# Four edits at the start of a decoder layer: the norm's row in a zeroed tile, filler products, the sample tile eighth, and each tile's sums behind the next tile's splits

## The chip, the core and the metric

The kernel runs on one core of a Trainium2 chip. The engines are PE (TensorE: products and transposes into PSUM), DVE (VectorE), ACT (ScalarE), POOL (GpSimd) and SP (SyncE, which here only issues loads). The metric is the device time of one execution in microseconds (us), as a median of runs.

## The reference

One layer of a recurrent decoder on 1024 new prompt tokens and 8 sample tokens. What matters here is its beginning:

```python
hn = rmsnorm(x, g_norm)                     # x * rsqrt(mean(x*x) + EPS) * g_norm, 1024 features
u = hn @ w_in                               # 1024 x 7176, in float32
xa, za, uq, uk, uv, uo, zb, ui, uf = jnp.split(u, SPLIT_IDX, axis=-1)
```

Then come an RG-LRU branch on `xa`, an mLSTM on `uq, uk, uv, ui, uf`, gates from `za, uo, zb`, a product with `w_out`, the residual and a last norm. Prompt and sample tokens go through the same weights; the sample has states of its own.

## The kernel before, in words

**Precision.** A float32 operand is split into two parts, `hi` (a cast on ACT, L72) and `lo = src - hi` (a subtraction on DVE, L73); `mm3` makes a product of three: hi x hi, hi x lo, lo x hi (L66 to L68).

**Token tiles.** The prompt's 1024 tokens are eight tiles of 128 (numbers 0 to 7), the eight sample tokens are tile 8. `xorder` sets the order, here 4, 0, 8, 5, 1, 6, 2, 7, 3. For each tile: `x_fetch` loads its 512 KB (the sample: 32 KB) three places ahead; `x_stats` (ACT's Square, a few small operations) makes the row scale; `x_turn` scales it by that and by the norm's gain `gn_b` on DVE (L439) and transposes it in eight 128x128 blocks on PE (L443); `x_split` splits the transposed halves (`b12` and `cb` of the page, for tiles 4 to 7 and 0 to 3); `plain` multiplies the tile with two groups of weight columns, w = 0 (with the gate columns, 264 wide, weights `wph`/`wpl`) and w = 1 (256 wide, `w1h`/`w1l`); and `x_combos` makes sums and differences of token halves and splits them too. They are the seven operand pairs `cb[q]` of a Strassen-like scheme (seven products of half-size blocks instead of eight), in which all other weight columns are multiplied. For the sample, `x_split` only copies the transposed tokens to `hnd`.

**The norm's row.** `g_norm` is loaded as one row, in two halves (`grow`), and spread to 128 partitions by a product with a column of ones (L537, one row deep, 512 columns each). The first tile takes it from PSUM, all others from the copy `gn_b`.

**Units.** The weight columns come in 14 units of 2 x 256 columns. A unit's raw weights are two buffers, `raw0` (rows 0 to 511) and `raw1`, of which there is one each: the next unit's load (`load_raw`, L244) must wait until the unit before has been read for the last time. Unit 0 is the one that `plain` multiplies. For every unit, `dec_unit` multiplies the sample (`hnd`) with the raw weights: eight products (L257) in a PSUM buffer `ps_tr`, of which there is one, then a copy `Z` on ACT. `prep` splits a unit's weights for one of the seven products (`wh`, `wl`), `product` makes it.

**Order.** The program is written in the order shown; a scheduler places each engine's instructions, and each engine then runs them strictly in order. `tc.issue_after(i)` keeps the instructions of a block behind `i` where they run on its engine. `dec_unit(0)` can run when `hnd` is there, so with the sample third it stands early. ACT and DVE run ahead with `prep` of unit 1 as soon as its raw weights are there.

Of the kernel before, what the change touches and what calls it, by code (L numbers as in the profile page):

```python
# [9 lines left out]
F32 = mybir.dt.float32  # L10
F32R = mybir.dt.float32r
BF16 = mybir.dt.bfloat16
AF = mybir.ActivationFunctionType
ALU = mybir.AluOpType
# [3 lines left out]
P = 128  # L18
T = 1024
HT = 512  # L20
NB = 8
KC = 8
# [29 lines left out]
def hymba_kernel(  # L52
# [7 lines left out]
    V, A, G, TE = nc.vector, nc.scalar, nc.gpsimd, nc.tensor  # L60
# [3 lines left out]
    def mm3(out, ah, al, bh, bl, first, last):  # L64

        TE.matmul(out, ah, bh, start=first, stop=False, skip_group_check=True)  # L66
        TE.matmul(out, ah, bl, start=False, stop=False, skip_group_check=True)  # L67
        TE.matmul(out, al, bh, start=False, stop=last, skip_group_check=True)  # L68

    def split(hi, lo, src):  # L70

        a = A.copy(hi, src)  # L72
        V.tensor_tensor(lo, src, hi.bitcast(F32), op=ALU.subtract)  # L73
        return a

    cpool = ctx.enter_context(tc.tile_pool(name="cpool", bufs=1))
    dram = ctx.enter_context(tc.tile_pool(name="dram", bufs=1, space=DRAM))
# [4 lines left out]
    def ps(tag, shape):  # L82
        return psp.tile(shape, F32, tag=tag, name=f"ps_{tag}", bufs=NBUF.get(tag, 1))

    def const(shape, name, dt=F32):
        return cpool.tile(shape, dt, tag=name, name=name)
# [14 lines left out]
    def sg(shape, name, dt=F32):  # L101

        return stg.tile(shape, dt, tag="stg", name=name)
# [4 lines left out]
    def dconst(shape, name):  # L108

        return dpool.tile(shape, F32, tag=name, name=name)  # L110
# [4 lines left out]
    ones = dconst([P, P], "ones")  # L115
# [102 lines left out]
    def blocks(t):  # L218
        return t[:, 0:KC * NB].rearrange("p (k b) -> p k b", b=NB)
# [164 lines left out]
        stq(d[t0:t0 + 256, :].rearrange("(i p) c -> p i c", p=P), t.rearrange("p (i c) -> p i c", i=2))  # L384


    grow = [sg([1, HT], f"grow{half}") for half in range(2)]
    for half in range(2):
        A.dma_start(grow[half], g_norm[:, half * HT:(half + 1) * HT])
    warm = const([P, 1], "warm")  # L390
    A.activation(warm, ones[:, 0:1], AF.Sqrt)
    es_f = ExitStack()
    fp = es_f.enter_context(tc.tile_pool(name="f_start", bufs=1))
    gn_b = fp.tile([P, T], F32, tag="gn_b", name="gn_b")
    xorder = [4, 0, 8, 5, 1, 6, 2, 7, 3]
    rows_of = lambda i: P if i < 8 else NB
    xt, xps, bf = {}, {}, {}

    def x_fetch(m):
        i = xorder[m]  # L400
        xt[i] = fp.tile([P, T], F32, tag="xb", name=f"x{i}") if m % 3 == 2 else ws([P, T], f"x{i}", F32)
        ld(xt[i][:rows_of(i)], x_prompt[0, i * P:(i + 1) * P, :] if i < 8 else x_sample[:, 0, :])
# [21 lines left out]
    def x_stats(i):  # L424
        n = rows_of(i)
        junk = fp.tile([P, T], BF16, tag="junk", name="junk")
        A.activation(junk[:n], xt[i][:n], AF.Square, accum_out=st0[:n, i, 0:1])
        rsqrt_mean(st0[:n, i, 1:2], st0[:n, i, 0:1], st0[:n, i, 2:3], T)

    def x_turn(m):  # L430
        i = xorder[m]
        n = rows_of(i)
        xps[i] = []
        for half in range(2):
            hs = slice(half * HT, (half + 1) * HT)
            if m == 0 or half == 0:
                s = hs if m == 0 else slice(0, T)
                g = pb[half] if m == 0 else gn_b[:n, s]
                scaled = V.scalar_tensor_tensor(xt[i][:n, s], xt[i][:n, s], st0[:n, i, 1:2], g, op0=ALU.mult, op1=ALU.mult)  # L439
            pt = ps(("kv", "kv", "s", "qp")[(2 * m + half) % 4], [P, 4, P])  # L440
            for q in range(4):
                k = half * 4 + q
                TE.transpose(pt[:, q, 0:n], xt[i][:n, k * P:(k + 1) * P], idF[:n, :n])  # L443
            xps[i].append(pt)
        del xt[i]
        return scaled

    def x_split(i, half):

        p = xps[i][half]  # L450
        if i == 8:
            V.tensor_copy(blocks(hnd)[:, 4 * half:4 * half + 4], p[:, :, 0:NB])
            return
        s = slice(i % 4 * P, (i % 4 + 1) * P)
        if i >= 4 and half == 0:
            bf[i] = [fp.tile([P, 4, P], F32R, tag=f"b12{n}", name=f"b12{n}") for n in "hl"]
            split(*bf[i], p)
        else:
            q = Q_P3 if i >= 4 else (Q_P1, Q_P2)[half]
            return split(cb[q][0][:, :, s], cb[q][1][:, :, s], p)  # L460

    def x_copy(i):

        bf["f"] = [sg([P, 4, P], f"b{n}2f") for n in (1, 2)]
        for f, p in zip(bf["f"], xps[i]):
            A.copy(f, p)

    def x_combos(i):

        p0, p1 = xps[i]  # L470
        s = slice(i % 4 * P, (i % 4 + 1) * P)
        f0, f1 = bf["f"]

        def out(q, t):
            split(cb[q][0][:, :, s], cb[q][1][:, :, s], t)
        if i >= 4:
            t3 = sg([P, 4, P], "t3")
            V.tensor_tensor(t3, f1, f0, op=ALU.subtract)
            out(Q_P7, t3)
        else:  # L480
            t1, t2, t4 = (sg([P, 4, P], f"t{n}") for n in (1, 2, 4))
            V.tensor_tensor(t1, f0, p0, op=ALU.subtract)
            V.tensor_tensor(t2, f1, t1, op=ALU.subtract)
            V.tensor_tensor(t4, p1, t2, op=ALU.subtract)
            out(Q_P6, t2)
            out(Q_P5, t1)
            out(Q_P4, t4)

    hi = fp.tile([P, KC, 264], F32R, tag="wph", name="wph")
    lo = fp.tile([P, KC, 264], F32R, tag="wpl", name="wpl")  # L490
# [3 lines left out]
    def w1_split(b):  # L494

        t = ws([P, 4, 256], f"w1h{b}"), ws([P, 4, 256], f"w1l{b}")
        split(t[0], t[1], raws[0, b][:, :, 256:512])
        w1.append(t)
# [3 lines left out]
    def plain(i):  # L502

        s = slice(i % 4 * P, (i % 4 + 1) * P)
        op = []
        for k in range(KC):
            if i < 4:
                op.append([t[:, k % 4, s] for t in cb[Q_P1 if k < 4 else Q_P2]])
            elif k < 4:
                op.append([t[:, k, :] for t in bf[i]])  # L510
            else:
                op.append([t[:, k % 4, s] for t in cb[Q_P3]])
        for w in range(2):
            pt = ps("o", [P, 512])[:, 0:264 - 8 * w]
            for k, (h, l) in enumerate(op):
                wh, wl = (hi[:, k, :], lo[:, k, :]) if w == 0 else (t[:, k % 4, :] for t in w1[k // 4])
                mm3(pt, h, l, wh, wl, k == 0, k == KC - 1)
            t = fp.tile([P, 256], F32, tag="pe", name="pe", bufs=2)
            A.copy(t, pt[:, 0:256])
            if w == 0:  # L520
                V.tensor_tensor(gs[:, i, :], pt[:, 256:264], bgate, op=ALU.add)
            stq(d_v[w][i * P:(i + 1) * P, :], t)

    pw = ps("tr", [P, P])
# [9 lines left out]
        TE.matmul(pw, ones, ones, start=True, stop=True)  # L534
    pb = [ps("o", [P, 512]) for half in range(2)]
    for half in range(2):
        TE.matmul(pb[half], ones[0:1, :], grow[half], start=True, stop=True)  # L537
    ld(wg, w_in[0, :, C_G:C_G + 8].rearrange("(k p) c -> p k c", p=P))
    load_raw(0, 1, (0,))
    x_fetch(1)  # L540
# [6 lines left out]
    for m, i in enumerate(xorder):  # L547
        scaled = x_turn(m)
        if m == 0:
            def w0_split(k):  # L550
                split(hi[:, k:k + 2, 0:256], lo[:, k:k + 2, 0:256], raws[0, k // 4][:, k % 4:k % 4 + 2, 0:256])
            with tc.issue_after(root.ins), tc.issue_after(scaled.ins):
                w0_split(0)
                split(hi[:, :, 256:264], lo[:, :, 256:264], wg)
                x_split(i, 0)
                w0_split(2)
            with tc.issue_after(x_split(i, 1).ins):
                w0_split(4)
                w0_split(6)
                for half in range(2):  # L560
                    A.copy(gn_b[:, half * HT:(half + 1) * HT], pb[half])
                x_stats(xorder[1])
                for b in range(2):
                    w1_split(b)
        else:
            x_split(i, 0)
            x_split(i, 1)
        if 4 <= i < 8:
            x_copy(i)
        if m + 3 < 9:  # L570
            x_fetch(m + 3)
        if m + 2 < 9:
            x_stats(xorder[m + 2])
        if i < 8:
            plain(i)
            x_combos(i)

    pgd = ps("o", [32, 8])
    for k in range(KC):
        TE.matmul(pgd, hnd[:, NB * k:NB * k + 32], wg[:, k, :], start=k == 0, stop=k == KC - 1)  # L580
# [1133 lines left out]
    for n in range(4, N):  # L1714
        c, h = n // 4, n % 4
# [90 lines left out]
```

## Time and profile before

| | |
|---|---|
| median of 3 runs | 925.69 us (924.45 to 925.9) |
| profiled execution, its own time | 923.33 us |
| its span, first to last instruction | 921.6 us |
| busy in the span: PE / DVE / ACT / POOL | 905.0 / 741.6 / 591.1 / 192.0 us |
| mean granted TensorE clock | 0.998 |

The page adds up the time in which an engine was at work. A PE row's end is modelled, so that the distance between the starts of two rows says more than a row's length. Each product in float32 (transposes, `dec_unit`, ones) is two instructions on PE. In the rows, `L257 PE MATMUL ps_tr<-raw,hnd` is line, engine, operation, what is written and what is read; `[0.81 <-DVE w1l L73]` says that the engine idled 0.81 us ahead of it and what ended that. Names are cut at their numbers: `x` is any token tile, `cb_hi` any of seven.

### The profile page before, as it was taken

The page shows a single profiled execution, that of the slowest core. Times are in us where ns is not written, and L with a number is a line of the kernel's source. Part 1 is how long each engine was busy: PE and PEld are TensorE (multiplying, and loading weights), DVE is VectorE, ACT ScalarE, POOL GpSimd, SP SyncE. Part 2 cuts the span into 40 slices and gives each one's busy share as a digit, 9 for nine tenths or more (in the row PEclk, how much of TensorE's full clock was granted, in tenths as well). Part 3 has the DMA queues.
Part 4 walks back from the last instruction along what each step waited for, and adds up shares of the span by engine and source line. Part 5 has one row for each costly group of instructions (what it writes and reads, how often), then busy time and mean ns, then how long its engine had stood idle before and what let it go on. Part 6 is the DMA issues. An engine that isn't in the chain of part 4 may idle for free.

```text
span 921.6 us, 15527 instructions
## 1 busy us (share of the span) xinstructions
PE 905.0 (98%) x5261; PEld 749.3 (81%) x5261; DVE 741.6 (80%) x1535; ACT 591.1 (64%) x1085; POOL 192.0 (21%) x317
## 2 busy tenths in 40 slices
PE   8999999999999999999999999999999999999997
PEld 6897777877687988787789898877778888778886
DVE  6874778888689878789888876679998779878873
ACT  7663456867667776576758775446876668656642
POOL 1111113112312222324333324010111110110120
PEclk9999999999999999999999999999999999999999
DMA  6611467456646566557765646436589798755642
GB/s 201 192 61 45 137 178 241 143 179 200 230 134 206 173 196 195 183 157 249 236 216 170 242 145 234 119 119 231 178 239 253 200 259 260 191 154 153 198 103 86
DMA packets 130600, 167.87 MB, mean 182 GB/s; under 512 B 17620, under 2 KB 98580, under 8 KB 130514
## 3 DMA queue, kind: packets, MB, share of 16 engines
q1 hardware_dynamic: 108934, 103.94, 37.4%
q0 software_dynamic: 21584, 62.95, 21.3%
q8 instruction: 41, 0.67, 0.3%
q14 instruction: 37, 0.30, 0.1%
q10 hardware_dynamic: 4, 0.00, 0.0%
HBM read 108.19 MB, written 62.92 MB: 186 GB/s over the span
## 4 chain that ended last, share of the span: by engine, by line
PE 88%; DVE 4%; ACT 3%; DMA 3%; issue 2%; POOL 0%; SPq 0%; DVEq 0%; ACTq 0%; POOLq 0%
PE ps_o L66 14%; PE ps_o L68 14%; PE ps_o L67 14%; PE ps_kv L66 10%; PE ps_kv L67 10%; PE ps_kv L68 10%; PE ps_tr L257 3%; PE ps_s L1198 2%; DMA Cb<-in_state_mlstm_C_dram 1%; DVE wl L73 1%; PE ps_qp L66 1%; PE ps_qp L67 1%; PE ps_qp L1016 1%; PE ps_qp L68 1%; PE ps_s L1200 1%
## 5 line engine op out<-in xcount | busy, mean ns | idle before, releaser
L72 ACT CAST wh<-raw 128x1024 fp32r<-128x1024 f32 x91 | 95.3, 1049 | 73.9 <-PE ps_o L67 27.7
L73 DVE TENSOR_TENSOR wl<-raw,wh 128x1024 fp32r<-128x1024 f32 x91 | 111.0, 1220 | 33.1 <-ACT wh L72 17.7
L66 PE MATMUL ps_kv<-cb_hi,wh 128*128 128x512 f32 x320 | 127.5, 398 | 0.0
L68 PE MATMUL ps_kv<-cb_hi,wl 128*128 128x512 f32 x320 | 125.3, 392 | 0.0
L67 PE MATMUL ps_kv<-cb_lo,wh 128*128 128x512 f32 x320 | 125.2, 391 | 0.0
L66 PE MATMUL ps_o<-cb_hi,wh 128*128 128x512 f32 x240 | 94.6, 394 | 0.0
L68 PE MATMUL ps_o<-cb_hi,wl 128*128 128x512 f32 x240 | 93.7, 390 | 0.0
L67 PE MATMUL ps_o<-cb_lo,wh 128*128 128x512 f32 x240 | 93.5, 390 | 0.0
L66 PEld LDWEIGHTS ps_kv<-cb_hi,wh 128*128 128x128 f32 x320 | 60.1, 188 | 21.4 <-issue 5.5
L67 PEld LDWEIGHTS ps_kv<-cb_lo,wh 128*128 128x128 f32 x320 | 60.2, 188 | 13.4 <-issue 1.7
L68 PEld LDWEIGHTS ps_kv<-cb_hi,wl 128*128 128x128 f32 x320 | 60.1, 188 | 12.9
L66 PE MATMUL ps_kv<-wh,cb_hi 128*128 128x256 f32 x192 | 55.3, 288 | 0.0
L67 PE MATMUL ps_kv<-wl,cb_hi 128*128 128x256 f32 x192 | 54.4, 283 | 0.0
L68 PE MATMUL ps_kv<-wh,cb_lo 128*128 128x256 f32 x192 | 54.3, 283 | 0.0
L66 PEld LDWEIGHTS ps_o<-cb_hi,wh 128*128 128x128 f32 x240 | 45.1, 188 | 10.0 <-issue 0.8
L66 PE MATMUL ps_o<-wo,mh 128*128 128x512 f32 (+1 forms) x136 | 53.1, 390 | 0.0
L68 PEld LDWEIGHTS ps_o<-cb_hi,wl 128*128 128x128 f32 x240 | 45.0, 188 | 9.8
L67 PEld LDWEIGHTS ps_o<-cb_lo,wh 128*128 128x128 f32 x240 | 45.1, 188 | 9.1
L68 PE MATMUL ps_o<-wo,ml 128*128 128x512 f32 (+1 forms) x136 | 51.7, 380 | 0.0
L67 PE MATMUL ps_o<-wo,mh 128*128 128x512 f32 (+1 forms) x136 | 51.5, 378 | 0.0
L66 PE MATMUL ps_o<-wh,cb_hi 128*128 128x256 f32 x144 | 40.9, 284 | 0.0
L67 PE MATMUL ps_o<-wl,cb_hi 128*128 128x256 f32 x144 | 40.7, 283 | 0.0
(550 smaller groups left out, 2601.6 us busy)
## 6 DMA issues: line engine op xcount, KB each, us to landing
raw<-in_w_in_dram SPq DMA_DIRECT2D x55, 512.0 KB
Cb<-in_state_mlstm_C_dram SPq DMA_DIRECT2D x32, 256.0 KB
out_dram<-Cb POOLq DMA_DIRECT2D x32, 256.0 KB, 4.7
qk<-d_qk SPq DMA_DIRECT2D x32, 256.0 KB
ring<-d_ro SPq DMA_DIRECT2D x28, 256.0 KB
d_qk<-s POOLq DMA_DIRECT2D x24, 256.0 KB, 4.5
d_x<-s POOLq DMA_DIRECT2D x16, 256.0 KB, 3.1
zsr<-d_y SPq DMA_DIRECT2D x16, 256.0 KB
```

Source lines behind the costliest of these rows:

```text
L66: TE.matmul(out, ah, bh, start=first, stop=False, skip_group_check=True)
L67: TE.matmul(out, ah, bl, start=False, stop=False, skip_group_check=True)
L68: TE.matmul(out, al, bh, start=False, stop=last, skip_group_check=True)
L72: a = A.copy(hi, src)
L73: V.tensor_tensor(lo, src, hi.bitcast(F32), op=ALU.subtract)
L257: TE.matmul(pz[32 * g:32 * g + 32, :], hnd[:, NB * k:NB * k + 32], raws[u, k // 4][:, k % 4, :], start=k < 4, stop=k >= 4, skip_group_chec ...
L1016: TE.matmul(pq[32 * g:32 * g + n, 0:256], q, ds_["C", h * NB + bb][:, kb, :], start=b == 1, stop=b == NB - 1, skip_group_check=True)
L1198: TE.matmul(S, qk[:, 2 + kb, :], qk[:, kb, :], start=kb == 0, stop=kb == 1)
L1200: TE.transpose(kn[:, kb * P:(kb + 1) * P], qk[:, 2 + kb, :], idF)
```

## The change

1. `grow` becomes two tiles of 128 rows, cleared by DVE, with `g_norm` in the first row; the spreading product reads all 128 rows of it and of `ones`. The loads of the row now come behind the clearing, and ACT's first activation behind the loads' issue.
2. `xorder` becomes 4, 0, 5, 1, 6, 2, 7, 8, 3: the sample is eighth.
3. In the first tile's w = 0 product, the two hi products of two blocks come first, then the two lo products; behind it stand six products of `ones` with `ones` whose result nobody reads. The cast and subtraction of the third and fourth block of `wph` come behind the first half's split.
4. `x_combos` of a tile comes behind `x_split` of the next one.

```diff
-        V.tensor_tensor(lo, src, hi.bitcast(F32), op=ALU.subtract)
-        return a
+        return a, V.tensor_tensor(lo, src, hi.bitcast(F32), op=ALU.subtract)
...
-    grow = [sg([1, HT], f"grow{half}") for half in range(2)]
+    grow = [sg([P, HT], f"grow{half}") for half in range(2)]
     for half in range(2):
-        A.dma_start(grow[half], g_norm[:, half * HT:(half + 1) * HT])
+        V.memset(grow[half], 0.0)
+        row = A.dma_start(grow[half][0:1, :], g_norm[:, half * HT:(half + 1) * HT])
     warm = const([P, 1], "warm")
-    A.activation(warm, ones[:, 0:1], AF.Sqrt)
+    with tc.issue_after(row.ins):
+        A.activation(warm, ones[:, 0:1], AF.Sqrt)
...
-    xorder = [4, 0, 8, 5, 1, 6, 2, 7, 3]
+    xorder = [4, 0, 5, 1, 6, 2, 7, 8, 3]
...
+            lows = []
             for k, (h, l) in enumerate(op):
                 wh, wl = (hi[:, k, :], lo[:, k, :]) if w == 0 else (t[:, k % 4, :] for t in w1[k // 4])
+                if i == xorder[0] and w == 0:
+                    TE.matmul(pt, h, wh, start=k == 0, stop=False, skip_group_check=True)
+                    TE.matmul(pt, h, wl, start=False, stop=False, skip_group_check=True)
+                    lows.append((l, wh))
+                    if k % 2:
+                        for a, b in lows:
+                            end = TE.matmul(pt, a, b, start=False, stop=k == KC - 1, skip_group_check=True)
+                        lows.clear()
+                    continue
                 mm3(pt, h, l, wh, wl, k == 0, k == KC - 1)
+            if i == xorder[0] and w == 0:
+                with tc.issue_after(end.ins):
+                    for _ in range(6):
+                        TE.matmul(pw, ones, ones, start=True, stop=True)
...
-        TE.matmul(pb[half], ones[0:1, :], grow[half], start=True, stop=True)
+        TE.matmul(pb[half], ones, grow[half], start=True, stop=True)
...
-                x_split(i, 0)
+                first = x_split(i, 0)
+            with tc.issue_after(first[0].ins), tc.issue_after(first[1].ins):
                 w0_split(2)
...
             x_split(i, 1)
+        if m and xorder[m - 1] < 8:
+            x_combos(xorder[m - 1])
...
             plain(i)
-            x_combos(i)
-
+
+    x_combos(xorder[-1])
     pgd = ps("o", [32, 8])
```

What this does to the engines' order, at three places. In the rows, a name's numbers are those of its buffer: `raw0_0` is unit 0's `raw0`, `raw0_1` is unit 1's in the same place. First, PE where the token tiles end and unit 1 begins (L580 and L598 are the sample's gate products, `ps_kv` the first product of unit 1). Before:

```order
L68 MATMUL ps_o_978<-w1h1_293,cb_lo1_191 128x256
L580 MATMUL ps_o_1018<-wg_214,hnd_112 32x8 x8
L257 MATMUL ps_tr_1059<-raw0_1_1041,hnd_112 32x512 x4
L257 MATMUL ps_tr_1059<-raw1_1_1044,hnd_112 32x512 x4
L66 MATMUL ps_kv_1076<-cb_hi0_188,wh1_0_1051 128x512
```

and now:

```order
L68 MATMUL ps_o_986<-w1h1_295,cb_lo1_191 128x256
L598 MATMUL ps_o_1026<-wg_216,hnd_112 32x8 x8
L256 MATMUL ps_tr_1038<-raw0_0_222,hnd_112 32x512 x3
L256 MATMUL ps_tr_1038<-raw1_0_235,hnd_112 32x512 x4
L66 MATMUL ps_kv_1084<-cb_hi0_188,wh1_0_1059 128x512
L67 MATMUL ps_kv_1084<-cb_lo0_189,wh1_0_1059 128x512
L256 MATMUL ps_tr_1067<-raw0_1_1049,hnd_112 32x512 x4
```

Before, the sample's products with unit 1 stood there, and those with unit 0 behind tile 0's; now seven of the eight with unit 0 stand there (the first stands ahead of tile 3's products), and those with unit 1 among unit 1's own. Second, SP's loads between the first ones and those of the gates' parameters. Before:

```order
L402 DMA x5_301<-in_x_prompt_dram 128x1024
L402 DMA x1_386<-in_x_prompt_dram 128x1024
L402 DMA x6_477<-in_x_prompt_dram 128x1024
L244 DMA raw0_1_1041<-in_w_in_dram 128x4x256 x2
L402 DMA x2_507<-in_x_prompt_dram 128x1024
L244 DMA raw1_1_1044<-in_w_in_dram 128x4x256 x2
L402 DMA x7_592<-in_x_prompt_dram 128x1024
L402 DMA x3_691<-in_x_prompt_dram 128x1024
L583 DMA d_gd_121<-gd_1027 8x8
```

and now:

```order
L403 DMA x7_578<-in_x_prompt_dram 128x1024
L403 DMA x8_677<-in_x_sample_dram 8x1024
L403 DMA x3_762<-in_x_prompt_dram 128x1024
L243 DMA raw0_1_1049<-in_w_in_dram 128x4x256
L601 DMA d_gd_121<-gd_1035 8x8
L243 DMA raw0_1_1049<-in_w_in_dram 128x4x256
L243 DMA raw1_1_1052<-in_w_in_dram 128x4x256 x2
L633 DMA dgb_1131<-d_gd_121 128x64
```

Unit 1's raw weights stood among the token tiles' loads; now they stand behind the last of them, and the store of the sample's gates between their halves. Third, DVE from the low part of tile 5's first half, `b12l`, to that of its second, `cb_lo5`. Before, from tile 5's scaling on:

```order
L439 SCALAR_TENSOR_TENSOR x5_301<-x5_301,st0_117,gn_b_211 128x1024
L207 RECIPROCAL st0_117<-st0_117 128x1
L189 TENSOR_SCALAR st0_117<-st0_117 128x1
L209 SCALAR_TENSOR_TENSOR st0_117<-st0_117 128x1
L213 RECIPROCAL st0_117<-st0_117 128x1
L207 RECIPROCAL st0_117<-st0_117 128x1
L439 SCALAR_TENSOR_TENSOR x1_386<-x1_386,st0_117,gn_b_211 128x1024
L209 SCALAR_TENSOR_TENSOR st0_117<-st0_117 128x1
L213 RECIPROCAL st0_117<-st0_117 128x1
L73 TENSOR_TENSOR b12l_498<-ps_s_487,b12h_497 128x512
L73 TENSOR_TENSOR cb_lo5_199<-ps_qp_492,cb_hi5_198 128x4x128
```

and now, the part that ends in the same low part (`b12l` of tile 5 stands six rows ahead of the first row here, behind tile 0's own low parts):

```order
L485 TENSOR_TENSOR t4_479<-ps_qp_381,t2_478 128x512
L212 RECIPROCAL st0_117<-st0_117 128x1
L536 TENSOR_TENSOR gs_217<-ps_o_403,bgate_91 128x8
L73 TENSOR_TENSOR cb_lo3_195<-t2_478,cb_hi3_194 128x4x128
L73 TENSOR_TENSOR cb_lo2_193<-t1_477,cb_hi2_192 128x4x128
L73 TENSOR_TENSOR cb_lo6_201<-t4_479,cb_hi6_200 128x4x128
L206 RECIPROCAL st0_117<-st0_117 128x1
L440 SCALAR_TENSOR_TENSOR x1_303<-x1_303,st0_117,gn_b_213 128x1024
L73 TENSOR_TENSOR cb_lo5_199<-ps_kv_466,cb_hi5_198 128x4x128
```

Before, both low parts of tile 5 came in a row, behind all sums of tile 0; now the first comes ahead of those sums and the second behind them and behind tile 1's scaling.

More of the change, by code (lines that the diff above doesn't have):

```diff
@@ L456, in x_split @@
             bf[i] = [fp.tile([P, 4, P], F32R, tag=f"b12{n}", name=f"b12{n}") for n in "hl"]
-            split(*bf[i], p)
+            return split(*bf[i], p)
         else:
@@ L554, in hymba_kernel @@
                 split(hi[:, :, 256:264], lo[:, :, 256:264], wg)
-                x_split(i, 0)
+                first = x_split(i, 0)
+            with tc.issue_after(first[0].ins), tc.issue_after(first[1].ins):
                 w0_split(2)
-            with tc.issue_after(x_split(i, 1).ins):
+            with tc.issue_after(x_split(i, 1)[0].ins):
                 w0_split(4)
```

## The prediction

> **What bounds the kernel now.** I read the engines' busy table first, then the busy time of four stretches at the start, because the order of instructions differs only there: behind the first products of weight unit 1 all five engines run the same rows as before.
>
> ```profile
> PE 905.0 (98%) x5261; PEld 749.3 (81%) x5261; DVE 741.6 (80%) x1535; ACT 591.1 (64%) x1085; POOL 192.0 (21%) x317
> ```
>
> ```profile
> 0.00:9.10 9.10, 7.97 (x23) 4.84 (x23) 3.33 (x10) 5.04 (x11) 2.10 (x12) 1.00 0.79 241
> 9.10:21.70 12.60, 10.51 (x69) 9.26 (x68) 10.66 (x23) 10.97 (x22) 1.13 (x2) 1.00 0.50 161
> 21.70:72.40 50.70, 50.20 (x418) 46.50 (x420) 40.04 (x84) 32.14 (x66) 7.03 (x13) 1.00 0.38 126
> 72.40:100.00 27.60, 27.60 (x140) 21.37 (x132) 13.81 (x24) 9.86 (x13) 1.87 (x5) 1.00 0.22 71
> ```
>
> The columns are the stretch, its length, and busy time of PE, PEld, DVE, ACT and POOL. PE is the bound of the whole. From 9.10 to 21.70 it lacks 2.1 us, from 21.70 to 72.40 only 0.5, and across the step from the token tiles to unit 1 (72.40 to 100) nothing. So the end moves by what PE idles less at the start, plus what it idles anew. PE's own rows of the start, in order of time (start, duration, and in brackets the wait):
>
> ```profile
> 3.57 3.78 PE L537 MATMUL ps_o<-grow,ones 1*128 1x512 f32 x4
> ...
> 12.41 0.42 PE L68 MATMUL ps_o<-wph,b12l 128*128 128x264 f32 x1
> 12.63 0.34 PE L66 MATMUL ps_o<-wph,cb_hi 128*128 128x264 f32 x1
> 12.80 0.28 PE L67 MATMUL ps_o<-wpl,cb_hi 128*128 128x264 f32 x1
> 12.92 0.28 PE L68 MATMUL ps_o<-wph,cb_lo 128*128 128x264 f32 x1
> ...
> 14.14 0.28 PE L66 MATMUL ps_o<-w1h,b12h 128*128 128x256 f32 x1
> 15.23 0.39 PE L67 MATMUL ps_o<-w1l,b12h 128*128 128x256 f32 x1 [0.81 <-DVE w1l L73]
> ...
> 18.20 0.28 PE L68 MATMUL ps_o<-w1h,cb_lo 128*128 128x256 f32 x1
> 18.82 0.66 PE L443 MATMUL ps_s<-idF,x 128*128 128x128 f32 x4 [0.34 <-DVE x L439]
> 19.31 0.60 PE L443 MATMUL ps_qp<-idF,x 128*128 128x128 f32 x4
> 20.46 0.39 PE L66 MATMUL ps_o<-wph,cb_hi 128*128 128x264 f32 x1 [0.55 <-ACT cb_hi L72]
> ...
> 21.14 0.66 PE L443 MATMUL ps_kv<-idF,x 8*128 8x8 f32 x8
> 21.72 0.39 PE L68 MATMUL ps_o<-wph,cb_lo 128*128 128x264 f32 x1
> ```
>
> Two things are to be seen. Equal products follow each other every 0.22 us up to 12.63 and every 0.12 from 12.80, though the granted clock stands at 1.00 in all stretches: up to 12.6 us PE runs at half rate. And it waits for `w1l`, for tile 0's scaling and for tile 0's casts, which ACT and DVE deliver in one unbroken chain:
>
> ```profile
> 7.38 0.75 DVE L439 SCALAR_TENSOR_TENSOR x<-x,st,ps_o 128x512 f32<-128x512 f32 x1 [0.63 <-PE ps_o L537]
> ...
> 16.76 0.69 DVE L478 TENSOR_TENSOR t<-b22f,b12f 128x512 f32<-128x512 f32 x1
> ...
> 17.50 1.26 DVE L439 SCALAR_TENSOR_TENSOR x<-x,st,gn_b 128x1024 f32<-128x1024 f32 x1
> ...
> 20.98 0.67 DVE L73 TENSOR_TENSOR cb_lo<-ps_s,cb_hi 128x512 fp32r<-128x512 f32 x1
> ```
>
> ```profile
> 8.43 0.59 ACT L72 CAST b12h<-ps_kv 128x512 fp32r<-128x512 f32 x1 [0.60 <-PE ps_kv L443]
> 9.34 0.59 ACT L72 CAST cb_hi<-ps_kv 128x512 fp32r<-128x512 f32 x1 [0.33 <-PE ps_kv L443]
> 9.82 1.14 ACT L72 CAST wph<-raw 128x512 fp32r<-128x512 f32 x2
> ```
>
> **The change, part by part.** *A, the start.* The product that spreads the norm's row takes as many columns as before, so at the same rate it costs the same 3.78. The first tile's clock is what it may move: with 128 rows at work instead of one, PE may reach full rate inside that product. The second scaling waits 0.63 for it at 7.38, and the first cast waits 0.60 at 8.43 for the transposes behind it; both waits then go, and `b12h` moves to about 8.43 - 0.60 = 7.8. One 512-column cast (0.5 from start to start, 9.34 to 9.82) now stands between `b12h` and `cb_hi`, in place of one ahead of `b12h`; so the pair at 9.82 comes at 7.8 + 3 x 0.5 = 9.3, 0.5 earlier, and the chain behind it with it. DVE then scales tile 0 directly behind `w1l`, at the place where 16.76 stands, not 17.50: 0.74 more. From that scaling to tile 0's low part it took 3.48 (17.50 to 20.98) with the sample's scaling between, and takes about the same with tile 5's scaling between, which is as long. Best case 0.5 + 0.74 = 1.2 off the product at 21.72. Against it stand two clearings of a 128x512 tile ahead of the row's loads (no row shows that size; between nothing and one 512-column DVE operation each, 0.75) and 512 KB of tile 5 instead of 32 KB of the sample in the first loads. I take 1.0, with bounds 1.2 and 0.
>
> The six fillers are twelve PE instructions, 1.4 us at 0.12 each. They stand where PE waits for `w1l` (14.14 to 15.23, and longer if the first products end sooner); that wait hides them, and without it they would cost up to 1.4. The reordered low products add none. While it waits for tile 0's low part, PE now transposes six of tile 5's eight blocks (19.31 to 20.46 less the wait: about 0.12 each, 0.7) instead of the sample's eight (21.14 to 21.72, 0.58): 0.1 gained.
>
> A rule of the Trainium skill speaks against the clock part: the page "TensorE: Matmul & The Clock Gate", Part 1, says that about 3.4 us of sustained matmuls release the half rate. The rows above show matmuls from 3.57 on and half rate at 12.41, so one-row products did not count here, or the rule would have released it long before; if any product counted alike, the 128 rows would change nothing, and A would be rival 2's 0.4 instead of 1.0.
>
> *B, 21.7 to 72.4.* At most the 0.5 that PE lacks there can be won. Something can be lost: the sample's product with unit 0 (below) filled PE in this stretch and has left it, DVE is busy 40.04 of 50.70, and on DVE tile 0's sums and tile 1's scaling now stand between the two low parts of tile 5. If PE, through with the first half, comes there before DVE, it waits; I bound that by one such scaling, 1.26. I take 0.2 gained, bounds 0.5 gained and 1.3 lost.
>
> *C, the step to unit 1.* The sample now comes eighth, so the eight products of the sample with unit 0's raw weights move from 27 us to the end of the token tiles. Unit 1's weights go into the same two buffers:
>
> ```profile
> 27.28 1.83 PE ps_tr L257 x10
> ...
> 37.97 3.86 DMA x<-in_x_prompt_dram
> ...
> 72.42 1.77 PE ps_tr L257 x14
> 74.19 0.43 PE ps_kv L66
> ```
>
> ```profile
> 28.38 0.94 SPq L244 DMA_DIRECT2D raw<-in_w_in_dram  x2
> ```
>
> ```profile
> SPq L244 <- PE ps_tr L257: 6.8, 2, 6.2
> ```
>
> ```profile
> L72 ACT CAST wh<-raw x91: 1027/1049/1060, 52.5 to 642.3; 128x1024 fp32r<-128x1024 f32 x91
> L73 DVE TENSOR_TENSOR wl<-raw,wh x91: 1160/1221/1227, 58.7 to 643.6; 128x1024 fp32r<-128x1024 f32 x91
> ```
>
> The first two fences are the chain of waits and SP's queue, the third what SP waited for, the last the durations of the splits. Before, unit 1's loads left at 28.38, right behind those products, 46 us ahead of the first product that needs them (74.19); nothing waits. Now the load cannot leave until the fourth of the eight products has read its buffer, and behind it PE has only the other four: eight instructions, of which 14 took 1.77 at 72.42, so 1.0. Then PE stands until the load has landed and ACT has cast it. A 512 KB load from issue to the work it frees took 3.86 (37.97); the cast takes 1.05; handing over I put at 0.05. The wait is 3.86 + 1.05 + 0.05 - 1.0 = 4.0. The bounds come from
>
> ```profile
> 28.00:30.00 2.00, 2.00 (x14) 0.97 (x9) 1.97 (x8) 0.46 (x2) 0.54 (x1) 1.00 0.31 68
> 32.00:34.00 2.00, 2.00 (x19) 2.00 (x18) 1.50 (x3) 1.07 (x2) 0.00 (x0) 1.00 1.08 386
> ```
>
> Almost nothing moved in the 1.6 us behind the issue at 28.38, and 386 GB/s is the best rate: 1.6 + 1.4 = 3.0, so a wait of 3.1 at least; the two halves of the load sharing the rate would land at 1.6 + 2.7 = 4.3, giving 4.4. [...]
>
> *D, behind it.* The sample's products with unit 1 now stand between unit 1's own; they are no new work. The second buffer's load leaves 1.0 later, and all four halves, 2.1 MB, need 1.6 + 5.4 = 7.0 us; PE gets to them about 7.7 after the first issue. DVE's split (1.22) follows the cast while PE has 1.4 of other work. I take 0.3 for this, bounds 0 and 1.5.
>
> Sum: -1.0 - 0.1 - 0.2 + 4.0 + 0.3 = +3.0. On the profiled execution's own 923.33 that is 926.3; that execution lies 2.4 below the median of the runs shown, 925.69, and the prediction is for such a median: 925.69 + 3.0 = 928.7. With all bounds at their ends the change is -1.2 - 0.1 - 0.5 + 3.1 = +1.3 to 0 - 0.1 + 1.3 + 4.4 + 1.5 = +7.1.
>
> **The rivals.** *1, the start pays for the wait.* All that PE could win ahead of unit 1 is its lack from 9.10 to 72.40 (2.1 + 0.5), the half rate's surplus (the first half's twelve products up to 12.63, 0.10 each, 1.2) and the waits of the first tile's head (0.63 and 0.33, 1.0): 4.8. If more than 2.4 of that is won against 4.0 + 0.3, the result is within 0.2% (1.85 us, about what a measurement of this kernel can tell from no change, used for all chances here). If nearly all is won and the load lands in 3.0, it is 4.8 - 3.1 = 1.7 faster, 924.0; the point from which it is not slower is a gain equal to the wait. For it: the trace shows all of this idle time. Against it: DVE and ACT, 10.66 and 10.97 of 12.60, bound the start and keep the same work. 26%, of it 8% faster by over 0.2%, mostly because one execution shows one moment of full rate only.
>
> *2, the clock does not come sooner:* all rows but one are zeros, and no row shows what those count for. Then `b12h` stays at 8.43, the pair comes at 8.43 + 1.5 = 9.93, 0.1 later than now, the clearings cost some 0.2, and of the 0.74 on DVE 0.4 is left: +3.6, 929.3. For it: the half rate held to 12.41 through every product ahead of it. Against it: those ahead of 8.43 had one row or were transposes. 18%.
>
> *3, the wait drags on:* both halves of the load share the queue, and the sample's sums of units 0 and 1, which share one PSUM buffer, wait for each other through ACT and DVE. 4.4 + 1.5 and nothing or a loss in B: +5.0 to +7.1, say 931.7. 7%.
>
> **How the numbers follow.** The forecast, +1.9 to +5, has 49%. The range goes from +0.6, inside rival 1, to +5.7, inside rival 3: 926.3 to 931.4. Slower by over 0.2%: 49 + 18 + 7 = 74%; within: 18%; faster: 8%.
>
> **What would show it.** Right: SP issues unit 1's first raw load behind the eighth tile's work, at about 70 us instead of 28; PE has one wait of about 4 us for the `wh` cast ahead of the first product of unit 1, with the load in it; PE's products are 0.12 apart before 10 us; the wait for `w1l` is gone or filled with the twelve fillers. Wrong: unit 1's first product comes at or before 74 us, or PE idles less than 2.5 us ahead of it; or PE waits more than 1.5 us in the token tiles behind 22 us, which would make it slower than said.

## The result, and the profile after

The changed kernel takes 942.61 us (median of five executions, 932.65 to 945.28) against 924.45 for the kernel before in the same comparison (923.69 to 925.9). The ratio is 1.0164, with a 95% interval of 1.0135 to 1.0192: 18 us slower where 3 were forecast. Note the spread: 13 us between executions of the changed kernel, 2 us before.

Where the 18 us lie is read off by following the same PE instruction through both traces (us from the start of the span):

| PE instruction | before | after | later by |
|---|---|---|---|
| tile 0's first product | 20.46 | 19.14 | -1.3 |
| last product of the token tiles | 71.57 | 70.47 | -1.1 |
| unit 1's first product | 74.12 | 77.22 | +3.1 |
| unit 1's second product | 80.73 | 87.55 | +6.8 |
| last product ahead of the last heads' transposes | 895.02 | 904.36 | +9.3 |
| last heads' transposes | 895.36 | 913.39 | +18.0 |
| end of the span | 921.6 | 940.8 | +19.2 |

PE's line of the page says little of it, 97% where it was 98%:

```profile
PE 909.0 (97%) x5273; PEld 751.6 (80%) x5273; DVE 743.8 (79%) x1537; ACT 589.0 (63%) x1085; POOL 191.9 (20%) x317
```

By the table there are two big places: the step to unit 1, which the prediction spoke of, and the last 45 us, of which it said nothing. Between them 2.5 us gather, 1.6 of them at one place. First PE's rows of the changed kernel at the start and at unit 1:

```profile
3.54 2.73 PE L552 MATMUL ps_o<-grow,ones 128*128 128x512 f32 x4
...
12.49 1.50 PE L532 MATMUL ps_tr<-ones 128*128 128x128 f32 x12
14.78 0.39 PE L67 MATMUL ps_o<-w1l,b12h 128*128 128x256 f32 x1 [0.67 <-DVE w1l L73]
19.14 0.39 PE L66 MATMUL ps_o<-wph,cb_hi 128*128 128x264 f32 x1 [0.24 <-ACT cb_hi L72]
...
29.66 0.39 PE L68 MATMUL ps_o<-wph,cb_lo 128*128 128x264 f32 x1 [0.53 <-DVE cb_lo L73]
...
77.22 0.80 PE L66 MATMUL ps_kv<-cb_hi,wh 128*128 128x512 f32 x1 [4.22 <-ACT wh L72]
```

The spreading product is done in 2.73 instead of 3.78, the twelve filler instructions take 1.50 ahead of the `w1l` wait, and unit 1's first product waits 4.22. The windows of the changed kernel beside those of the forecast (length, then PE, PEld, DVE, ACT, POOL busy, granted clock, DMA share, GB/s):

```profile
21.70:70.50 48.80, 47.00 (x380) 44.68 (x378) 38.26 (x82) 27.49 (x61) 7.03 (x13) 1.00 0.23 73
...
73.00:77.20 4.20, 0.00 (x0) 0.00 (x0) 0.01 (x1) 1.63 (x2) 0.00 (x0) 0.95 0.93 282
...
76.80:80.20 3.40, 2.98 (x10) 0.70 (x10) 1.23 (x1) 1.19 (x2) 0.00 (x0) 0.50 0.98 315
80.20:83.60 3.40, 3.40 (x21) 1.88 (x18) 3.23 (x3) 0.80 (x2) 0.00 (x0) 1.00 0.01 2
```

PE lacks 1.8 us in the token tiles, where it lacked 0.5, and behind the wait it has only half the clock for 3.4 us. It has half the clock once more at 824 us, behind a wait of 2.1 us. The kernel before has that wait too, of 2.3 us, and keeps its clock there (first the changed kernel, then the kernel before):

```profile
824.30:827.70 3.40, 3.40 (x13) 2.96 (x12) 2.66 (x8) 1.18 (x3) 0.00 (x0) 0.50 0.27 89
816.80:820.20 3.40, 3.40 (x20) 2.90 (x19) 3.33 (x11) 2.22 (x5) 0.00 (x0) 1.00 0.47 155
```

Ahead of that stretch PE is 7.5 us later than before, behind it 9.1. The chain of waits has the load and the cast of the forecast, and at the end a piece that the kernel before does not have:

```profile
71.35 0.83 PE ps_tr L256 x4
72.23 3.87 DMA raw<-in_w_in_dram
76.12 1.05 ACT wh L72
77.22 0.80 PE ps_kv L66
...
890.14 19.32 DMA so<-d_so
```

`so` is the output gate of one head and one token tile (128 KB): `m_g` multiplies the head's result by it (L1276 before, L1294 now). The last head's is loaded at 890.14, and what needs it starts at 909.48 (first before, then after):

```profile
891.44 0.43 DVE L1276 SCALAR_TENSOR_TENSOR hh<-so,hh 128x256 f32<-128x256 f32 x1 [0.77 <-DMA so<-d_so]
909.48 0.42 DVE L1294 SCALAR_TENSOR_TENSOR hh<-so,hh 128x256 f32<-128x256 f32 x1 [9.48 <-DMA so<-d_so]
```

PE's longest wait is behind that:

```profile
PE ps_s L1321 <- ACT hh L1312: 8.6, 1, 8.6
```

SP's queue shows both loads, first before, then after (start, time that the issue took):

```profile
879.27 0.37 SPq L1170 DMA_DIRECT2D z<-d_zs  x1
880.81 0.32 SPq L1165 DMA_DIRECT2D so<-d_so  x1
```

```profile
888.61 0.37 SPq L1188 DMA_DIRECT2D z<-d_zs  x1
890.14 2.68 SPq L1183 DMA_DIRECT2D so<-d_so  x1
```

Both issues stand 9.3 us later than before, as all else does, but the issue itself took 2.68 us instead of 0.32. What the DMA engines did around it, first before, then after:

```profile
881.00:885.00 4.00, 4.00 (x28) 3.65 (x27) 3.77 (x9) 2.53 (x7) 1.35 (x3) 1.00 0.10 27
...
889.50:892.50 3.00, 3.00 (x16) 2.54 (x15) 2.16 (x8) 0.51 (x2) 1.42 (x2) 1.00 1.13 395
892.50:898.00 5.50, 5.50 (x28) 4.20 (x27) 4.25 (x16) 3.76 (x11) 1.12 (x2) 1.00 0.88 84
```

```profile
892.00:896.00 4.00, 4.00 (x25) 3.48 (x24) 3.51 (x11) 2.87 (x9) 1.42 (x2) 1.00 0.25 36
...
899.00:902.00 3.00, 3.00 (x16) 2.50 (x15) 0.97 (x4) 0.00 (x0) 1.42 (x2) 1.00 1.09 390
902.00:904.00 2.00, 2.00 (x11) 1.65 (x10) 0.00 (x0) 0.00 (x0) 0.00 (x0) 1.00 1.67 122
904.00:909.00 5.00, 0.75 (x4) 0.29 (x2) 0.00 (x0) 0.00 (x0) 0.00 (x0) 1.00 0.85 30
```

The traffic is clogged twice in both kernels: first behind the load of `z` (27 and 36 GB/s, with 640 KB waiting), then, after three microseconds at 390 to 395 GB/s, a second time, with the engines busy and little moved. Before, `so` was there at 891.44, a microsecond ahead of the second clog; DVE had waited 0.8 for it and PE not at all. Now it is caught in the second clog. What lies beside SP's long issue is in the DMA queues of 888.5 to 891.5:

```profile
q14 instruction: 1, 0.01, 7.5%
```

One load of 8 KB of program code, which took 7.5% of 3 us of 16 engines, so 3.6 us. In the same place of the kernel before there is none, and all of its loads of this queue together are on its page as

```profile
q14 instruction: 37, 0.30, 0.1%
```

37 of them in 0.1% of 16 engines' 921.6 us, so some 0.4 us each.

The other traces agree. In four of them (the changed kernel and the runs below with the sample eighth alone, with 16 fillers, and with two more ACT operations) a code load begins 1.2 us ahead of the issue of the last `so` and takes 2.7 to 3.6 us. SP's issue then takes 1.8 to 2.7 us and ends 0.3 us behind the load. In the five in which the last code load comes 9 to 10.5 us behind that issue (the kernel before and the runs with the norm's row alone, with 36 fillers and, twice, with the sample third), the issue takes 0.32.

### The profile page after: what moved, and what is told of

Its sections match the earlier page's. It is cut to its first block, busy times and chain, and to the rows that moved or that the text cites. A ratio compares the mean times of both kernels' runs of the same rounds, so it can differ in the third digit from the quotient of the medians.

```text
span 940.8 us, 15556 instructions
## 1 busy us (share of the span) xinstructions
PE 909.0 (97%) x5273; PEld 751.6 (80%) x5273; DVE 743.8 (79%) x1537; ACT 589.0 (63%) x1085; POOL 191.9 (20%) x317
## 4 chain that ended last, share of the span: by engine, by line
PE 65%; issue 16%; DMA 7%; DVE 6%; ACT 3%; POOL 3%; SPq 0%; POOLq 0%; DVEq 0%; ACTq 0%
PE ps_o L66 10%; PE ps_o L68 9%; PE ps_o L67 9%; PE ps_kv L66 9%; PE ps_kv L67 9%; PE ps_kv L68 9%; PE ps_tr L256 2%; DMA so<-d_so 2%; POOL d_p L1448 1%; DMA Cb<-in_state_mlstm_C_dram 1%; DMA x<-in_x_prompt_dram 1%; DVE wl L73 1%; PE ps_tr L264 1%; PE ps_tr L845 1%; PE ps_s L845 1%
## 5 line engine op out<-in xcount | busy, mean ns | idle before, releaser
L66 PE MATMUL ps_o<-wo,mh 128*128 128x512 f32 (+1 forms) x136 | 54.2, 399 | 0.0
L67 PE MATMUL ps_o<-wo,mh 128*128 128x512 f32 (+1 forms) x136 | 52.4, 385 | 0.0
L68 PE MATMUL ps_o<-wh,cb_lo 128*128 128x256 f32 x144 | 40.8, 283 | 0.0
```

## Experiments: the start

The edits by themselves, to see what the front is worth. First the changed kernel with the sample back in third place:

```diff
-    xorder = [4, 0, 5, 1, 6, 2, 7, 8, 3]
+    xorder = [4, 0, 8, 5, 1, 6, 2, 7, 3]
```

> The changed kernel with the sample back as third tile, the other three edits kept. If the late raw weights make the step to unit 1 dear, PE no longer waits 4.2 us for the first cast of unit 1, PE's clock stays up behind it, and unit 1's first product starts at 74.1 within 1.5. If the other edits were the cost, it starts at 77 still. For the end: if the 8.6 us wait of PE for the last head's scaling comes from being late at unit 1, it is gone and the time is 924 within 1.5; if it comes from the other three edits, or by chance, it is there and the time is about 933.

926.93 us against 926.0, ratio 1.0013 (1.0000 to 1.0026). No wait at unit 1, whose first product starts within 0.1 us of where it did, no wait at the end. (I had expected 924 within 1.5; the kernel before too was slower in this comparison.) So the three other edits cost nothing much and bring nothing: the 18 us hang on the sample's place. Tile 0's first product came at 19.06, 1.4 earlier than before, but at 29.2 PE waits:

```profile
29.20 0.63 PE L444 MATMUL ps_s<-idF,x 128*128 128x128 f32 x4 [1.09 <-DVE st L208]
```

The wait is 1.09, for the next tile's row scale, and that tile's first product starts at 31.18, where before it was 31.25. What was won at the front was won on PE; DVE, which makes scales, scalings and low parts, is not ahead by as much, and PE meets it at the next tile.

The kernel before with the norm's row in a zeroed tile alone:

```diff
-    grow = [sg([1, HT], f"grow{half}") for half in range(2)]
+    grow = [sg([P, HT], f"grow{half}") for half in range(2)]
...
+        V.memset(grow[half], 0.0)
...
-        TE.matmul(pb[half], ones[0:1, :], grow[half], start=True, stop=True)
+        TE.matmul(pb[half], ones, grow[half], start=True, stop=True)
```

> The kernel before with the first edit alone (the norm's row in a zeroed tile of 128 rows). If the 128 rows bring PE's full rate sooner, equal products stand 0.12 us apart from about 9 us on instead of 12.8, tile 0's products come some 0.5 us earlier, and the time is 0.3 to 0.5 us less than before: 923.8. If the clearing and the later loads eat it, 0 to +0.3. The end is as before, without the late wait.

925.51 us, ratio 1.0000 (0.9982 to 1.0017). The rate did come sooner:

```profile
9.95 0.28 PE L66 MATMUL ps_o<-wph,b12h 128*128 128x264 f32 x1
10.07 0.28 PE L67 MATMUL ps_o<-wpl,b12h 128*128 128x264 f32 x1
10.18 0.28 PE L68 MATMUL ps_o<-wph,b12l 128*128 128x264 f32 x1
```

Products of this size stand 0.12 apart at 9.95, where before they stood 0.22 apart up to 12.63. At 14.1 PE was 0.8 ahead of before, and the last product of the token tiles still starts 0.76 earlier (70.81 for 71.57); in the time at the end nothing of it can be told.

The changed kernel with the sample third and the sums in their old place (first and third edit alone), and the same with `so` of the last head loaded one head earlier:

```diff
-    xorder = [4, 0, 5, 1, 6, 2, 7, 8, 3]
+    xorder = [4, 0, 8, 5, 1, 6, 2, 7, 3]
...
-        if m and xorder[m - 1] < 8:
-            x_combos(xorder[m - 1])
...
             plain(i)
-
-    x_combos(xorder[-1])
+            x_combos(i)
+
```

The second run's further edit is that of the last run below.

> The changed kernel with the sample third and each tile's sums in their old place: only the first edit and the order of the first tile's products and fillers are left. The 1.4 us won at tile 0's first product should now last, if the moved sums were what ate it (with the sample third and the sums moved, it was gone at 29 us): 1 to 1.4 us faster than before. If the first tiles' chain on DVE takes it back anyway, within 0.5 of before.

> The same with the last head's output gate loaded one head earlier. In the kernel before this load lands in time, so the median should be that of the kernel without it, within 1 us; the few slow executions of the kernel before (929.1 against 923.7) should be missing if they come from that load.

924.94 us, ratio 0.9998 (0.9979 to 1.0018), and 924.82 us, ratio 0.9998 (0.9979 to 1.0017). An interval of 1.6 to 1.9 us to either side is too wide for the 1 to 1.4 us that I expected, so the traces have to tell. Tile 0's first product starts at 20.36 and 19.81, where it was 20.46 before and 19.06 with the sums moved. So 0.75 to 1.3 of the 1.4 came from moving the sums (the prediction's 0.74 is this part), and that is what is gone at the next tile. The rest, 0.1 and 0.65, is kept: the last product of the tiles is 0.12 and 0.79 earlier than before. It ends at 251 us, where PE waits for ACT: 1.40 before, 2.03 and 2.32 in these two and 1.94 with the norm's row alone, and behind it the clock is at 0.50 for 3.4 us in two of the three, which it is not before. So my expectation was wrong, because the sums bring most of the 1.4 themselves, and the rival is wrong as well, because DVE's chain does not take the rest back. The second expectation was half wrong: the median is the same, but single executions of up to 929.27 are still there (up to 929.93 of the kernel before), so the spread of the kernel before does not come from that load. No version here is shown to be faster than the kernel before.

## Experiments: the step to unit 1

The kernel before with the sample eighth and nothing else:

```diff
-    xorder = [4, 0, 8, 5, 1, 6, 2, 7, 3]
+    xorder = [4, 0, 5, 1, 6, 2, 7, 8, 3]
```

> The kernel before with only the sample put eighth. The load's wait should be there alone: about 4.0 us ahead of unit 1's first product, then some 1.7 us at half rate, no loss in the token tiles: +5.7, 930.2 us. If the late wait at the end is tied to a late unit 1, 8 to 9 us more, about 939. Rival (the other three edits carry a part of the +6.8 at unit 1): the step costs less than 5 here.

938.66 us, ratio 1.0137 (1.0086 to 1.0189). One line of the change makes almost all of its loss, the wait at the end included:

```profile
PE ps_s L1303 <- ACT hh L1294: 6.6, 1, 6.6
PE ps_kv L66 <- ACT wh L72: 4.3, 1, 4.3
...
PE ps_o L68 <- DVE cb_lo L73: 1.4, 2, 0.8
```

The wait for the load is 4.3, as forecast. Waits for a low part (`cb_lo`) are there without the moved sums too, 1.4 here and 1.3 in the changed kernel: 0.6 at 36.4 us for tile 1's here, 0.5 at 29.7 for tile 5's there, and 0.8 for tile 7's in both. With the sample's tile and its products with unit 0 gone from between, PE comes to the low parts before DVE. Unit 1's second product is 8.1 us later than before, not 5.7: in this execution the half clock lasted two stretches of 3.4 us,

```profile
75.90:82.70 6.80, 5.14 (x15) 2.46 (x16) 3.21 (x3) 2.09 (x2) 0.00 (x0) 0.50 0.69 224
```

PE has no other wait between 72 and 90 us, here as in the changed kernel.

Now the changed kernel with 16 fillers in that wait:

```diff
     dec_unit(0)
+    pf_ = ps("o", [P, P])
+    for _ in range(16):
+        TE.matmul(pf_, ones, ones, start=True, stop=True)
     load_raw(1, 0)
```

> The changed kernel with 16 filler products (32 instructions, some 4.0 us) in PE's wait for unit 1's first cast. The load's wait stays as long (first product of unit 1 at 77.2), but if the half rate behind it is due to the idle time, PE runs at full rate at once, and unit 1's second product begins at 85.9 instead of 87.6: 1.7 us less. If the half rate has another cause, it stays at 87.6. The end is as in the changed kernel: 938 to 943, or 931 where the late load is in time.

```profile
72.71 3.84 PE L605 MATMUL ps_o<-ones 128*128 128x128 f32 x32
76.97 0.50 PE L66 MATMUL ps_kv<-cb_hi,wh 128*128 128x512 f32 x1 [0.42 <-ACT wh L72]
```

```profile
77.20:81.50 4.30, 4.30 (x22) 2.40 (x21) 3.25 (x3) 1.06 (x1) 0.00 (x0) 1.00 0.63 206
```

The first product comes at 76.97, 0.25 earlier than without fillers, as the tiles' last product does (0.22). But the clock stays full, and unit 1's second product begins at 85.95 instead of 87.55. From the first to the second product it takes 8.98 instead of 10.33: 1.4 of the 6.8 us were the half clock, and it was the idle time that brought it. The end is untouched: 939.86 us, ratio 1.0167 (1.0143 to 1.0190), PE's last wait 7.3.

## Experiments: the end

Is it lateness that makes the late wait? The kernel before with 36 fillers ahead of unit 1:

```diff
     dec_unit(0)
+    pf_ = ps("o", [P, P])
+    for _ in range(36):
+        TE.matmul(pf_, ones, ones, start=True, stop=True)
     load_raw(1, 0)
```

> The kernel before with 36 filler products (72 instructions at 0.12 us) ahead of the sample's products with unit 1: everything behind them is 8.6 us later, as in the changed kernel, and nothing else differs. If lateness as such brings the wait at the end, PE waits about 9 us for the last head's scaling and the time is 924.5 + 8.6 + 9 = 942; if it is the state that the queues are left in at unit 1, or chance, the time is 933.

934.12 us, ratio 1.0087 (1.0069 to 1.0106). PE's wait at the end is 0.4:

```profile
888.78 0.32 SPq L1168 DMA_DIRECT2D so<-d_so  x1
```

So being late is not it: 8 us later and all in order. Is it the clog? The changed kernel without the four small stores that stand among the last heads (it leaves out one of the outputs, the new mLSTM vector state):

```diff
-            stq(p_n[0, 0, h].rearrange("(kb p o) -> p kb o", p=P, o=1), mx["Cf"][h][:, :, 256:257])
```

> The changed kernel without the four stores of the new mLSTM vector state (1 KB each in single elements), which are left out. If these small stores hold up the queues at the end, the last head's load lands in about 10 us as before instead of 19, PE does not wait for the last head's scaling, and the time is 942.6 - 9.3 = 933. If other traffic holds them up (the matrix states of 256 KB, the stores of y), the wait of about 8.6 us stays and the time is 940 to 945.

933.64 us, ratio 1.0080 (1.0059 to 1.0102), no wait at the end. The code load is in the same place, just ahead of the issue of `so`, but takes 0.5 us, and the issue 0.32. Behind the load of `z` the engines now move 213 GB/s, where it was 36 in the changed kernel with the stores:

```profile
892.70:896.70 4.00, 4.00 (x27) 3.59 (x26) 3.77 (x10) 1.89 (x6) 1.13 (x2) 1.00 0.72 213
```

Four stores of 1 KB, written as single elements, clog the queues for all others. But the kernel before has them too. What differs is the load of code, and the next two runs move that. ACT's program has the same length in the kernel before, in the one with the sample third and in the one with 36 fillers; in the changed kernel it is two instructions longer, with the sample eighth alone one (all instructions of the trace are counted, those for waiting too). So first the kernel before with two more tiny operations at its very start:

```diff
-    A.activation(warm, ones[:, 0:1], AF.Sqrt)
+    for _ in range(3):
+        A.activation(warm, ones[:, 0:1], AF.Sqrt)
```

> The kernel before with two more tiny ACT operations at its start (the warming operation three times), nothing else. In the two kernels with the late wait at the end, one load of 8 KB of instructions began just ahead of the last head's load and took over 3 us, SP needed 2.2 and 2.7 us instead of 0.3 to issue that load, and ACT's program was one and two instructions longer than in the kernels without the wait. If the place of that code load decides, it moves here as in the changed kernel, though nothing is late: PE waits some 6 to 9 us for the last head's scaling and the time is 931 to 935. If it was chance, or the sample's place in another way, the time is 924 to 927.

928.96 us, ratio 1.0036 (1.0010 to 1.0062). Of all engines' programs only ACT's is longer here. SP's queue, the code load of 880.9 to 883.4, and PE's wait in the profiled execution:

```profile
882.45 2.03 SPq L1166 DMA_DIRECT2D so<-d_so  x1
```

```profile
q14 instruction: 1, 0.01, 7.5%
```

```profile
PE ps_s L1304 <- ACT hh L1295: 4.8, 1, 4.8
```

Nothing is late in this kernel, nothing of the change is in it, and it has the whole signature. It is not as dear as I had expected (931 to 935): its ten executions lie between 922.31 and 932.02, so the load is probably caught in some and not in others; only one of them has a trace. Then the changed kernel with 16 small copies on ACT, in the wait of unit 1:

```diff
-        A.copy(Z, pz)
+        cp = A.copy(Z, pz)
...
+        return cp
...
-    dec_unit(0)
+    with tc.issue_after(dec_unit(0).ins):
+        for _ in range(16):
+            A.copy(warm, ones[:, 0:1])
```

> The changed kernel with 16 tiny ACT copies in the wait of unit 1, where ACT is idle. If the place of the code load decides, it now comes some 8 us earlier, in front of the clogged stretch; SP issues the last head's load in 0.3 us, the wait at the end is gone and the time is 942.6 - 9.3 = 933. If not, it stays at 940 to 945.

933.67 us, ratio 1.0092 (1.0067 to 1.0118), and no wait at the end: more instructions, 9 us less.

```profile
892.51 0.32 SPq L1186 DMA_DIRECT2D so<-d_so  x1
```

```profile
q14 instruction: 1, 0.01, 5.7%
```

The code load now lies in 886 to 889 (5.7% of 16 engines there, 2.7 us), ahead of both issues. Last, the changed kernel with that one load a head earlier, into a staging buffer:

```diff
-            sos[n] = mx["p"].tile([P, 256], F32, tag="so", name="so", bufs=2)
+            sos[n] = sg([P, 256], "so") if n == 4 * NCH - 1 else mx["p"].tile([P, 256], F32, tag="so", name="so", bufs=2)
...
-        so_load(n)
+        if n < N - 1:
+            so_load(n)
+        if n == N - 2:
+            so_load(n + 1)
```

> The changed kernel with the last head's output gate loaded one head earlier, into a buffer of the staging pool. If the load that lands too late is all that PE waits for at the end, that wait is gone whatever the code load does: 933, and a spread of 2 us in place of 13. If the queues would hold up something else instead (the loads of y for the last tiles), it is 936 or more.

932.48 us, ratio 1.0086 (1.0064 to 1.0109), four executions between 931.0 and 933.2, no wait at the end, though a code load of 2.8 us is at the same place. So the late `so` is all that PE waits for there, and most of the changed kernel's spread of 13 us comes from it. What is left without it, 0.86%, is 8 us: the step to unit 1 and the small steps behind.

## Why the prediction was right and wrong, step by step

**A, the start: right.** Forecast -1.1 with the fillers hidden. The trace has -1.3 at tile 0's first product and -0.9 at the product at 21.72 that the forecast named (20.86 now), the products 0.12 apart from 8.9, and the fillers in the `w1l` wait. Its two parts are seen apart as well: without the moved sums 0.1 and 0.65 are won at tile 0's first product (0.5 in the forecast), the rest with them (0.74 there). Rival 2 (the clock does not come sooner) is refuted, by the run with that edit alone too.

**B, the token tiles: wrong in sign.** I took 0.2 gained, with 1.3 lost as the bound. Seven of the sample's eight products with unit 0 left the stretch. Eight are worth 1.87 (16 instructions from 72.25 to 74.12 before), so seven 1.64. The last product of the tiles is only 1.1 earlier, so the tiles' own work ends 0.5 later, where A and B together should have made it 1.3 earlier: 1.8 missed. Of this 0.2 is A's, and B lost 1.4 instead of winning 0.2. One part is that the front's gain did not hold where the sums were moved (the run with the sample third: -1.4 at 19.06, nothing at 31.2). The other is that the sample's leaving let PE run into DVE (the run with the sample eighth: the tiles' own work ends 1.64 - 0.82 = 0.8 later, with nothing won at the front). I had named the second and given it no weight, and I had booked A's gain as if it were kept to the end. The sign that I gave for this, more than 1.5 us of waits in the tiles, is what the windows show: 1.8.

**C, the load: right.** Forecast 4.0 from 3.86 + 1.05 + 0.05 - 1.0; measured 4.22 from 3.87 + 1.05, with SP's load leaving at 72.23 instead of 28.38.

**D, behind it: mis-sized.** 0.3 taken, bound 1.5. Of the 6.8 us at unit 1's second product, A and B make 0.5 and C 4.2, which leaves 2.1 for D. The half clock alone is 1.4 of it in the profiled execution; no run takes the other 0.7 apart. The mechanism was missing: I had read in the start's rows that PE begins at half rate, and did not ask whether 4 us of idling would bring that back. The Trainium skill's page "TensorE: Matmul & The Clock Gate", Part 1, which I had cited for the start, says that it does: an idle window of about 3.4 us halves the clock, and the window runs freely. The trace agrees, 0.50 from 76.8 to 80.2 here and twice as long in the run with the sample eighth. But a wait need not be that long here: one of 2.1 us was enough at 824.

**Rival 1** (the start pays for the wait) fell because no more than 1.3 of its 4.8 was won, and that was not kept. **Rival 3** (the wait drags on, +5.0 to +7.1) had 7% and comes near this part's number, 6.8, but by luck. The loss in B is as it says. Its wait is not: PE waits once between 72 and 90 us, for 4.2, and not at all for the sums of units 0 and 1; what came on top was the clock.

**The end: not in the prediction at all.** I wrote that behind unit 1's first products all engines run the same rows as before, and took that to mean the same times. The order is the same; the phase of the code loads is not, and neither is anything that is won or lost in a race. This is the step that failed most. Of the 18 us some 7 to 10 are this: 0.0164 - 0.0086 of 925 is 7 by the medians, and 18.0 - 9.3 = 8.7, with 1.2 of half clock behind it, in the profiled execution. Another 1.6 are the half clock at 824, behind a wait that both kernels have.

**Left open.** That the code load is ACT's is argued from two things only: its place moved with the length of ACT's program, in the run with two more instructions and in the one with sixteen. How far it moves is not in proportion. Against the issue of `z` it lies 11.6 us behind in the kernel before, 0.3 behind with two more instructions and 4.4 ahead in the changed kernel with 16 copies. That SP's issue ends 0.3 us behind the code load was seen in four traces; why it does, and why single-element stores clog the queues for 10 us, was not tried. Why the clock fell at 824 behind a wait of 2.1 us, and not before behind one of 2.3, stays open. The other 0.9 of the 2.5 us between unit 1 and the end stand at waits that other executions have at other sizes.

## What to carry to other kernels

A gain counts only up to the next place where the engine meets the one that feeds it: ask of each microsecond won on PE whether the other engine is ahead by as much there. A new wait of some microseconds costs more than its length if PE's clock falls in it; fillers in the wait give that part back. And where a load lands just in time for its use, any edit, even two tiny instructions elsewhere, can make it miss: look for such loads in the trace of before (here DVE's 0.8 us for `so`), and issue them earlier before judging other edits by the time.

## What the runs showed of the hardware

- A load of 8 KB of code, on average 0.4 us, took 2.7 to 3.6 us among the last heads, and 0.5 without the four small stores there; an issue of SP that fell into it took 1.8 to 2.7 us instead of 0.32. The Trainium skill's page "Runtime: NRT & Kernel Launch", Instruction fetch mechanics, calls the cost of such loads mostly hidden; here one cost 5 to 9 us.
- Stores of 1 KB in single elements, one per head, held the queues at 27 to 36 GB/s with 640 KB waiting; without them it was 213.
- PE's half clock is lifted by products of 128 rows, also where 127 of the rows are zeros (equal products 0.12 apart from 9 us), and not by products of one row (from 3.57) or by transposes (from 7.28), which left it to 12.6. It comes back in a wait of 4.2 us, and 3.84 us of fillers prevent it; a wait of 2.1 us brought it back in one trace, and one of 2.3 at the same place in another did not.
- Two more tiny ACT operations at the start made a kernel of 924 us slower by 0.36% (0.10 to 0.62%).
